# A decoder trunk on one core: the mLSTM gate chain spread over early column pairs, two sums in place, other last pairs, and the first head's q and k split before the head stage

## The chip, the core and the metric

The kernel runs on one core of a Trainium2 chip. A core has TensorE (PE, matmuls), VectorE (DVE), ScalarE (ACT), GpSimd (POOL) and SyncE (SP), which issues nearly all DMAs of this kernel. Each engine works through its own instructions in order and waits on semaphores for the others. The metric is the device time of one execution in microseconds; the number shown for a kernel is the median of several executions.

## What is computed

One layer of a hybrid trunk on 512 tokens of width 2048, in float32:

```python
x = x + mixer(rms_norm(x, norm_mix0))
x = x + swiglu_ffn(rms_norm(x, norm_ffn0))
return rms_norm(x, final_norm)

def mlstm_retention_mixer(h, w_in, b_gates, w_conv, g_ml, g_ret, w_out):
    proj = h @ w_in                     # 2048 x (8 * 1024 + 8)
    ml_qk, ml_v, ml_o, r_q, r_k, r_v, r_g, gates = split(proj)
    ml_qk = silu(causal_conv(ml_qk, w_conv))
    i_pre, f_pre = split(gates + b_gates)
    h_ml = mlstm_chunkwise(ml_q, ml_k, ml_v, i_pre, f_pre)        # 4 heads of 256
    h_ml = head_norm(h_ml, g_ml) * sigmoid(ml_o)
    h_ret = retention_chunkwise(rotary(r_q), rotary(r_k), r_v)    # 4 heads of 256
    h_ret = head_norm(h_ret, g_ret, center=True) * silu(r_g)
    return concat(h_ml, h_ret) @ w_out
```

The gates of the mLSTM go through a log-sigmoid, a cumulative sum in each chunk of 128 tokens, and a running maximum over the chunks.

## The kernel before

All matrices are held transposed: 128 channels on the partitions, 512 tokens along the free dimension. A float32 product is made of fp32r parts: `split` (L80) writes a weight tile's rounded half `whi` with a cast on ACT (L84) and the rest `wlo` with a subtraction on DVE (L85).

**Projection.** `w_in` is taken in 32 column pairs of 256 columns. The pair number says what it holds: 0 to 3 mLSTM q, 4 to 7 mLSTM k, 8 to 11 mLSTM v, 12 to 15 the output gate (normed, sigmoid), 16 to 19 retention q and 20 to 23 retention k (rotary), 24 to 27 retention v, 28 to 31 the retention gate (normed, Silu). Two pairs go plainly with the gate columns; the other 30 go through `strassen` (L198), in the order of the list in L291. Such a pair takes seven products of 16 matmuls (A11, A12, S2, S1, S3, S4, A22; L209, L210, L213), in PSUM banks a, b and c. The weights of a product are a block as loaded (`b11`, `b21`, `b12`, `b22`) or a sum that `added` (L220) makes: q1, t2, t4, t3. S3 accumulates on top of S2's bank, which ACT has copied out at L246 by then. The results are collected on ACT and DVE (L241 to L261); `done` (L429) scales, rotates or gates them and stores them to a scratch tensor `pd` in HBM.

`r4` (L63) gives tiles of 512 KB from a pool of ten slots, which all of this shares: blocks, sums, the tables of cosine and sine, the gates' tiles, and later the residual stream.

**Gates.** `gates` (L371), behind the last pair, is a chain of small operations on 4 partitions: bias, |f|, exp, ln, a correction with a reciprocal (L388), scans for each chunk (L402 to L407), an exponential (L411), two stores of rows, and four PE transposes (L416), whose results are copied into `cols` (L421).

**Heads.** Four retention heads and four mLSTM heads follow. A retention head loads k, q, v and its gate from `pd` (`load`, L486; tiles `ld` with four buffers, or `ahead` for the first head), splits k and q (`two_parts`, L508), transposes v on PE and scales it on ACT (L503), and makes scores (L528), which DVE multiplies by a decay table `dec` (L615). Two banks `tp` serve both transposes and scores. The numerators (L544) are copied out on ACT (L626). Output-projection steps (`residual_gemm`, L129) are filled in between. The tiles of the head stage lie where the projection's operands lay, so they can be written only when the last pairs have been multiplied.

**Order.** The code is written in program order, but a scheduler lists the instructions of each engine by its own reckoning of priorities, slots and durations. The order in which instructions stand on an engine is therefore read from the built program.

Of the kernel before, what the change touches and what calls it, by code (L numbers as in the profile page):

```python
# [33 lines left out]
WU = 1024  # L34
# [4 lines left out]
def trunk(ctx: ExitStack, tc: tile.TileContext, xT, xr, w_in, w_gate, w_out, w_gu, w_down, w_pairs,  # L39
# [23 lines left out]
    def r4(shape, dtype=F32):  # L63
        return rp.tile(shape, dtype, name="r4")
# [133 lines left out]
    def strassen(j, src, cbs, ep, psp, done, between=None):  # L198
# [21 lines left out]
        def added(x, y):  # L220
            t = r4([P, WU])[:, 0:n_k * P]
            nc.vector.tensor_add(t, x, y)  # L222
            return t
# [23 lines left out]
        t4 = added(t2, b21)  # L247
        product(c, split(q1), S1, True)
        nc.scalar.copy(two[:, 0], c)
        t3 = added(b12, b22)  # L250
# [32 lines left out]
    xq = xT.rearrange("(n q p) t -> q p n t", n=2, p=P)  # L283
    pd = dram.tile([32, P, 2, T], F32, name="pd")
    rows = dram.tile([2, NH, T], F32, name="rows")
    with ExitStack() as proj:
# [4 lines left out]
        order = [24, 25, 26, 27, 16, 0, 4, 20, 8, 1, 5, 17, 2, 9, 6, 21, 3, 10, 18, 7, 28, 11, 22, 29, 30, 19, 31, 12, 23, 13, 14, 15]  # L291
# [79 lines left out]
        def gates():  # L371
            space = [r4([36, 2, T]) for _ in range(3)]
            st = space[0][:, 0, :]
            e, u, lg, d, f = (x[0:NH, n, :] for x, n in ((space[0], 1), (space[1], 0), (space[1], 1),
                                                         (space[2], 0), (space[2], 1)))
            gsum = gate_rows[0]
            fr, ig = gsum, gsum[0:NH, :]
# [6 lines left out]
            nc.scalar.activation(e, e, AF.Exp, scale=-1.0)  # L384
            nc.vector.tensor_scalar_add(u, e, 1.0)
            nc.scalar.activation(lg, u, AF.Ln)
            nc.vector.scalar_tensor_tensor(out=d, in0=u, scalar=-1.0, in1=e, op0=ALU.add, op1=ALU.subtract)
            nc.vector.reciprocal(u, u)  # L388
            nc.vector.tensor_mul(d, d, u)
            nc.vector.tensor_sub(lg, lg, d)  # L390
            lf = e
            nc.vector.scalar_tensor_tensor(out=lf, in0=f, scalar=0.0, in1=lg, op0=ALU.min, op1=ALU.subtract)

            b, c, m = f, u, lg
            carry = const.tile([NH, NC + 1], F32, name="carry", tag="warm")
            nc.vector.memset(carry, 0.0)

            nc.gpsimd.memset(st, 0.0)
            for i in range(NC):
                s = slice(i * CH, (i + 1) * CH)  # L400
                last = slice((i + 1) * CH - 1, (i + 1) * CH)
                nc.vector.tensor_tensor_scan(out=b[:, s], data0=ones[0:NH, :], data1=lf[:, s], initial=0.0,  # L402
                                             op0=ALU.mult, op1=ALU.add)
                nc.vector.tensor_sub(c[:, s], ig[:, s], b[:, s])
                nc.vector.tensor_tensor_scan(out=m[:, s], data0=c[:, s], data1=c[:, s],
                                             initial=carry[:, i:i + 1], op0=ALU.max, op1=ALU.max)
                nc.vector.tensor_add(carry[:, i + 1:i + 2], b[:, last], m[:, last])  # L407
            nc.vector.tensor_copy(st[0:NH, :], c)
            bm = d
# [3 lines left out]
            nc.sync.dma_start(out=rows[1], in_=b)  # L413
            tp = psp.tile([P, T], F32, name="aux")
# [54 lines left out]
        all_pairs([(w_in[n], stored(n)) for n in order[2:]], cbs, ep, psp, {0: normalise}, plain_done)  # L469
        gates()  # L470
# [7 lines left out]
    with ExitStack() as mix:  # L478
        hp = mix.enter_context(tc.tile_pool(name="hp", bufs=1, reuse_waits="tile"))
        ahead = {}  # L480
        for n in (20, 16, 24):
            ahead[n] = r4([P, 2, T])
            nc.sync.dma_start(out=ahead[n], in_=pd[n])
# [24 lines left out]
        def two_parts(t, name):  # L508
            hi, lo = (hp.tile([P, 2, T], F32R, name=name + x, bufs=2) for x in "hl")
            nc.scalar.copy(hi, t)  # L510
            nc.vector.tensor_tensor(out=lo, in0=t, in1=hi.bitcast(F32), op=ALU.subtract)
            return hi, lo
# [93 lines left out]
        def retention_head(h, pool, out):  # L606
            kT = two_parts(load(20 + h), "kT")
            qT = two_parts(load(16 + h), "qT")
# [297 lines left out]
```

## Time and profile before

| | us |
|---|---|
| median of three runs | 2297.26 |
| lowest and highest | 2295.38, 2298.49 |
| the profiled execution | 2298.28 |
| its span, first to last instruction | 2296.2 |

| engine | busy us of the span |
|---|---|
| PE | 2252.6 (98%) |
| DVE | 2004.8 (87%) |
| ACT | 1177.2 (51%) |
| POOL | 45.2 (2%) |

Times in views are microseconds from the span's start. The projection's pairs run until about 660, the heads until about 920, then the FFN. In a table of stretches each engine has its busy time and count, then the granted clock of PE as a share of full speed and the share of the DMA engines. In a timeline a row has a start, a length, and in brackets how long the engine stood idle before it and what released it. Matmuls are pipelined: a row's length is longer than the step to the next row.

### The profile page before, as it was taken

Reading aid. Unit: us, or ns where it says so; the run is one execution under the profiler, and the core shown is the slowest. Engines: PE = TensorE matmul, PEld = TensorE weight load, DVE = VectorE, ACT = ScalarE, POOL = GpSimd, SP = SyncE. Lnnn points to the kernel's source line nnn. Section 1 sums busy time; section 2 is a strip of 40 time slices with the busy share of each in tenths; the row PEclk is TensorE's granted clock in tenths of the full one; section 3 lists DMA queues with packets and bytes.
Section 4 is the critical chain, followed back from the end, with each engine's and each line's share of the span. In section 5 each row is a group of like instructions: output and inputs, shape, how many; then the busy total and the mean of one; then the engine's idle time right before and its main releaser. Section 6 shows DMA issues by size and latency. Waiting matters only on the chain.

```text
span 2296.2 us, 31553 instructions
## 1 busy us (share of the span) xinstructions
PE 2252.6 (98%) x12264; PEld 1937.6 (84%) x12264; DVE 2004.8 (87%) x2454; ACT 1177.2 (51%) x1569; POOL 45.2 (2%) x48
## 2 busy tenths in 40 slices
PE   9999999999989999799999999999999999999997
PEld 7888888888878888688888888888888888888887
DVE  6898988989987976999899999999999899898685
ACT  6544444545567744554545445454445545545233
POOL 0000000000000001300000000000000000000000
PEclk9999999999999999999999999999999999999999
DMA  8444334443374523333333333333333664864752
GB/s 267 155 139 137 130 129 130 137 137 128 130 243 160 159 92 122 144 122 117 117 123 124 124 124 121 114 115 124 124 116 120 209 229 149 270 204 150 271 205 74
DMA packets 140806, 343.59 MB, mean 150 GB/s; under 512 B 12264, under 2 KB 60648, under 8 KB 140656
## 3 DMA queue, kind: packets, MB, share of 16 engines
q1 hardware_dynamic: 140656, 341.57, 45.0%
q8 instruction: 96, 1.57, 0.3%
q14 instruction: 54, 0.44, 0.1%
HBM read 288.03 MB, written 53.49 MB: 149 GB/s over the span
## 4 chain that ended last, share of the span: by engine, by line
PE 90%; DVE 5%; DMA 2%; ACT 2%; issue 1%; POOL 1%; SPq 0%; DVEq 0%; POOLq 0%; ACTq 0%
PE a L210 27%; PE c L210 14%; PE a L213 12%; PE b L210 7%; PE c L213 6%; PE b L213 3%; PE mm L91 3%; PE mm L89 3%; PE mm L90 3%; PE a L209 2%; PE c L209 1%; DVE wlo L85 1%; PE c L89 1%; PE c L90 1%; PE c L91 1%
## 5 line engine op out<-in xcount | busy, mean ns | idle before, releaser
L210 PE MATMUL a<-cb,whi 128*128 128x512 f32 x2572 | 926.9, 398 | 4.0 <-DVE cb L155 4.0
L213 PE MATMUL a<-cb,wlo 128*128 128x256 f32 x2242 | 630.6, 281 | 0.5 <-DVE wlo L85 0.4
L210 PEld LDWEIGHTS a<-cb,whi 128*128 128x128 f32 x2572 | 480.0, 189 | 92.6 <-DVE cb L155 4.6
L85 DVE TENSOR_TENSOR wlo<-r,whi 128x1024 fp32r<-128x1024 f32 (+1 forms) x412 | 491.5, 1195 | 58.5 <-ACT whi L84 56.5
L84 ACT CAST whi<-r 128x1024 fp32r<-128x1024 f32 (+1 forms) x412 | 424.6, 1032 | 104.7 <-PE b L210 60.6
L210 PE MATMUL c<-cb,whi 128*128 128x512 f32 x1280 | 465.7, 397 | 0.2 <-ACT whi L84 0.2
L213 PEld LDWEIGHTS a<-cb,wlo 128*128 128x128 f32 x2242 | 424.5, 189 | 17.2 <-DVE wlo L85 2.2
L84 ACT CAST whi<-raw 128x1024 fp32r<-128x1024 f32 (+1 forms) x234 | 242.4, 1036 | 331.8 <-PE c L210 126.4
L85 DVE TENSOR_TENSOR wlo<-raw,whi 128x1024 fp32r<-128x1024 f32 (+1 forms) x234 | 281.2, 1202 | 38.0 <-ACT whi L84 37.5
L213 PE MATMUL c<-cb,wlo 128*128 128x256 f32 x1116 | 313.0, 280 | 0.0
L210 PEld LDWEIGHTS c<-cb,whi 128*128 128x128 f32 x1280 | 240.9, 188 | 44.0 <-ACT whi L84 0.6
L222 DVE TENSOR_TENSOR r<-r,r 128x1024 f32<-128x1024 f32 (+1 forms) x184 | 215.7, 1173 | 20.1 <-DMA r<-in_w_gu 17.2
L210 PE MATMUL b<-cb,whi 128*128 128x512 f32 x628 | 229.7, 399 | 0.0
L213 PEld LDWEIGHTS c<-cb,wlo 128*128 128x128 f32 x1116 | 210.8, 189 | 7.3 <-DVE wlo L85 0.2
L213 PE MATMUL b<-cb,wlo 128*128 128x256 f32 x548 | 154.4, 282 | 0.8 <-DVE wlo L85 0.8
L210 PEld LDWEIGHTS b<-cb,whi 128*128 128x128 f32 x628 | 118.9, 189 | 21.8
L261 DVE TENSOR_TENSOR e<-e 128x512 f32<-128x512 f32 x180 | 123.5, 688 | 9.2 <-ACT e L258 7.3
L258 ACT COPY e<-a 128x512 f32<-128x512 f32 x90 | 52.9, 588 | 146.1 <-PE a L210 146.1
L246 ACT COPY e<-a 128x512 f32<-128x512 f32 x90 | 53.0, 588 | 143.9 <-PE a L210 136.8
L222 DVE TENSOR_TENSOR r<-raw,r 128x1024 f32<-128x1024 f32 (+1 forms) x90 | 105.7, 1175 | 6.5 <-DMA r<-in_w_gu 2.9
L213 PEld LDWEIGHTS b<-cb,wlo 128*128 128x128 f32 x548 | 104.2, 190 | 4.5 <-DVE wlo L85 1.1
L89 PE MATMUL mm<-hi,whi 128*128 128x512 f32 x256 | 101.4, 398 | 3.2 <-DVE r L139 2.9
(289 smaller groups left out, 3350.1 us busy)
## 6 DMA issues: line engine op xcount, KB each, us to landing
r<-in_w_gu SPq DMA_DIRECT2D x89, 512.0 KB, 4.1
raw<-in_w_gu SPq DMA_DIRECT2D x87, 512.0 KB, 3.2
raw<-in_w_in SPq DMA_DIRECT2D x67, 512.0 KB, 3.5
r<-in_w_in SPq DMA_DIRECT2D x61, 512.0 KB, 3.7
raw<-in_w_down SPq DMA_DIRECT2D x40, 512.0 KB, 4.4
pd<-e SPq DMA_DIRECT2D x64, 256.0 KB, 2.7
raw<-in_w_out SPq DMA_DIRECT2D x32, 512.0 KB, 3.3
ld<-pd SPq DMA_DIRECT2D x29, 512.0 KB, 4.1
```

The source lines that it names most:

```text
L84: nc.scalar.copy(hi, raw)
L85: nc.vector.tensor_tensor(out=lo, in0=raw, in1=hi.bitcast(F32), op=ALU.subtract)
L89: nc.tensor.matmul(acc, wh, xh, start=first, stop=False)
L90: nc.tensor.matmul(acc, wh, xl, start=False, stop=False)
L91: nc.tensor.matmul(acc, wl, xh, start=False, stop=last)
L209: nc.tensor.matmul(*small, start=False, stop=False, skip_group_check=not first)
L210: nc.tensor.matmul(acc, wh[:, ks], cbs[k][:, c, :, :], start=(first and k == 0), stop=last, skip_group_check=not first)
L213: nc.tensor.matmul(*small, start=False, stop=False, skip_group_check=not first)
L222: nc.vector.tensor_add(t, x, y)
L246: nc.scalar.copy(two[:, 1], a)
L258: nc.scalar.copy(one[:, 0], a)
L261: nc.vector.tensor_add(x[:, :, 0, :], x[:, :, 0, :], x[:, :, 1, :])
```

## The change

- `gates` is cut into seven pieces, which are called between products of pairs 0, 2 to 10 of the 30 (`between`, L251); its reciprocal is made in two halves and its scans in two halves. The operations are the same.
- `added` may write into one of its inputs: t4 overwrites t2 and t3 overwrites b12.
- The order of pairs changes: 12 to 15 take the places of 9, 10, 11 and so on, so that the last two pairs are 10 and 11, which are stored as they are.
- The first head's k (pair 20) and q (pair 16) are loaded and split into `r4` tiles before the projection's pools close, and its v (pair 24) is loaded there.

```diff
-        def added(x, y):
-            t = r4([P, WU])[:, 0:n_k * P]
+        def added(x, y, into=None):
+            t = r4([P, WU])[:, 0:n_k * P] if into is None else into
             nc.vector.tensor_add(t, x, y)
             return t
...
-        t4 = added(t2, b21)
+        t4 = added(t2, b21, t2)
...
-        t3 = added(b12, b22)
+        t3 = added(b12, b22, b12)
...
-        order = [24, 25, 26, 27, 16, 0, 4, 20, 8, 1, 5, 17, 2, 9, 6, 21, 3, 10, 18, 7, 28, 11, 22, 29, 30, 19, 31, 12, 23, 13, 14, 15]
+        order = [24, 25, 26, 27, 16, 0, 4, 20, 8, 1, 5, 17, 2, 12, 6, 21, 3, 13, 18, 7, 28, 9, 22, 29, 30, 19, 31, 14, 23, 15, 10, 11]
...
-            nc.vector.reciprocal(u, u)
+
+        def gates_3(n):
+            half = gs["u"][:, n * HT:(n + 1) * HT]
+            nc.vector.reciprocal(half, half)
...
-            for i in range(NC):
+        def gates_5(n):
+            lf, b, c, m, ig, carry = (gs[x] for x in ("e", "f", "u", "lg", "ig", "carry"))
+            for i in range(2 * n, 2 * n + 2):
...
-        all_pairs([(w_in[n], stored(n)) for n in order[2:]], cbs, ep, psp, {0: normalise}, plain_done)
-        gates()
+        all_pairs([(w_in[n], stored(n)) for n in order[2:]], cbs, ep, psp,
+                  {0: normalise, 2: gates_1, 3: gates_2, 4: lambda: gates_3(0), 5: lambda: gates_3(1), 6: gates_4,
+                   7: lambda: gates_5(0), 8: lambda: gates_5(1), 9: gates_6, 10: gates_7}, plain_done)
+
+        for n in (20, 16):
+            x, hi, lo = r4([P, 2, T]), r4([P, 2, T], F32R), r4([P, 2, T], F32R)
+            nc.sync.dma_start(out=x, in_=pd[n])
+            nc.scalar.copy(hi, x)
+            nc.vector.tensor_tensor(out=lo, in0=x, in1=hi.bitcast(F32), op=ALU.subtract)
+            first_parts[n] = hi, lo
+        ahead[24] = r4([P, 2, T])
+        nc.sync.dma_start(out=ahead[24], in_=pd[24])
...
-        ahead = {}
-        for n in (20, 16, 24):
-            ahead[n] = r4([P, 2, T])
-            nc.sync.dma_start(out=ahead[n], in_=pd[n])
...
-            kT = two_parts(load(20 + h), "kT")
-            qT = two_parts(load(16 + h), "qT")
+            kT = first_parts.get(20 + h) or two_parts(load(20 + h), "kT")
+            qT = first_parts.get(16 + h) or two_parts(load(16 + h), "qT")
```

How the built programs stand at three places. First ACT at the end of the projection, in the kernel before (e_5705 and e_5706 are the results of the last pair, r_5830 the gates' tile, kTh and qTh the casts of k and q):

```order
L84 CAST whi<-raw 128x1024 x2
L258 COPY e_5705<-a 128x512
L446 ACTIVATE e_5706<-e_5706 128x2x256
L510 CAST kTh<-r_5889 128x1024
L411 ACT_TABLE_LOAD
L411 ACTIVATE r_5830<-r_5832 4x512
L446 ACT_TABLE_LOAD
L446 ACTIVATE e_5705<-e_5705 128x2x256
L510 CAST qTh<-r_5891 128x1024
L503 ACTIVATE v<-tp,rs 128x128 x8
```

and in the changed kernel (e_5699 is a result of the last pair, L528 what L503 was, L535 what L510 was, L651 what L626 was):

```order
L84 CAST whi<-raw 128x1024 x2
L258 COPY e_5699<-a 128x512
L84 CAST whi<-raw 128x1024
L528 ACTIVATE v<-tp,rs 128x128 x8
L535 CAST kTh<-ld 128x1024
L535 CAST qTh<-ld 128x1024
L651 COPY hn<-num 128x256 x2
```

The exponential, the sigmoids, the two casts and the table loads no longer stand between the last copy and the scaling of v; a weight cast does.

Second the DMA queue of SP at the same place, before (L490 loads for heads, L427 stores of the last pair, L612 decay tables, L654 residual, L75 weights of the output projection):

```order
L75 DMA raw<-in_w_out 128x1024
L412 DMA rows<-r_5831 4x512
L490 DMA ld<-pd 128x1024
L427 DMA pd<-e_5706 128x2x256
L612 DMA dec<-in_decay 128x512
L490 DMA ld<-pd 128x1024 x2
L427 DMA pd<-e_5705 128x2x256
L490 DMA ld<-pd 128x1024
L612 DMA dec<-in_decay 128x512
```

and changed (L515 loads for heads, L446 stores, L637 decay tables, L679 residual):

```order
L679 DMA r_6159<-in_xT 128x2x512
L75 DMA raw<-in_w_out 128x1024
L446 DMA pd<-e_5700 128x2x256
L75 DMA raw<-in_w_out 128x1024
L446 DMA pd<-e_5699 128x2x256
L515 DMA ld<-pd 128x1024
L637 DMA dec<-in_decay 128x512
L515 DMA ld<-pd 128x1024 x3
L637 DMA dec<-in_decay 128x512 x2
```

The first load for a head and the first decay table now stand behind both stores of the last pair, and the value load of the second head no longer stands behind one of them.

Third PE in a pair, at the end of product S2 (bank a) and the start of S1 (bank c), as it stands there in the kernel before:

```order
L209 MATMUL a<-cb,wlo 128x256
L210 MATMUL a<-cb,whi 128x512
L210 MATMUL c<-cb,whi 128x512
L213 MATMUL c<-cb,wlo 128x256
L210 MATMUL c<-cb,whi 128x512
```

and in pair 10 of the changed kernel (L435 is what L416 was):

```order
L209 MATMUL a<-cb,wlo 128x256
L210 MATMUL a<-cb,whi 128x512
L210 MATMUL c<-cb,whi 128x512
L435 MATMUL aux<-ident,r_1017 128x36 x4
L210 MATMUL a<-cb,whi 128x512
L213 MATMUL c<-cb,wlo 128x256
L210 MATMUL c<-cb,whi 128x512
```

Here the first matmul of S3 (bank a again) stands before the rest of S1; it does so in pairs 1, 3 and 27 too, there without L435 between.

## Rows read from the trace of the kernel before

**Rows 1.** The page, busy time and share of the span by engine.

```profile
PE 2252.6 (98%) x12264; PEld 1937.6 (84%) x12264; DVE 2004.8 (87%) x2454; ACT 1177.2 (51%) x1569; POOL 45.2 (2%) x48
```

**Rows 2.** Stretches: length, busy (count) of PE, PEld, DVE, ACT, POOL, clock, DMA.

```profile
110.00:300.00 190.00, 190.00 (x1079) 164.89 (x1078) 173.91 (x184) 90.15 (x107) 0.00 (x0) 1.00 0.42 140
...
640.00:660.00 20.00, 19.88 (x112) 16.76 (x111) 19.97 (x36) 11.67 (x15) 0.14 (x2) 1.00 0.71 217
...
664.00:672.00 8.00, 6.18 (x21) 5.13 (x22) 3.08 (x6) 7.21 (x14) 0.00 (x0) 0.50 0.94 329
```

**Rows 3.** Timeline of PE from the last projection matmul to the third head.

```profile
659.53 0.39 PE L210 MATMUL a<-cb,whi 128*128 128x512 f32 x1
664.44 0.64 PE L416 MATMUL aux<-ident,r 36*128 36x36 f32 x4 [4.52 <-ACT r L411]
665.01 1.97 PE L501 MATMUL tp<-ident,r 128*128 128x128 f32 x8
668.36 0.80 PE L89 MATMUL tp<-qTh,kTh 128*128 128x512 f32 x1 [1.39 <-ACT v L503]
...
676.83 0.50 PE L89 MATMUL tp<-qTh,kTh 128*128 128x512 f32 x1 [0.36 <-ACT v L503]
...
687.92 1.03 PE L501 MATMUL tp<-ident,ld 128*128 128x128 f32 x8
```

**Rows 4.** Chain that ended last, 655 to 700: start, step, what.

```profile
657.13 1.14 DVE wlo L85
658.27 0.60 DVE e L256
...
691.38 0.23 PE tp L90
...
692.71 0.17 PE tp L90
...
693.72 0.12 PE tp L90
```

**Rows 5.** Timeline of ACT, in a pair and behind the last one.

```profile
648.99 0.59 ACT L246 COPY e<-a 128x512 f32<-128x512 f32 x1 [1.21 <-PE a L210]
...
659.96 0.59 ACT L258 COPY e<-a 128x512 f32<-128x512 f32 x1 [1.76 <-PE a L210]
...
662.46 1.28 ACT L411 ACT_TABLE_LOAD   x1
663.75 0.63 ACT L411 ACTIVATE r<-r 4x512 f32<-4x512 f32 x1
...
667.17 2.17 ACT L503 ACTIVATE v<-tp,rs 128x128 f32<-128x128 f32 x8
669.85 1.05 ACT L510 CAST kTh<-ld 128x1024 fp32r<-128x1024 f32 x1 [0.51 <-DMA ld<-pd]
671.15 1.05 ACT L510 CAST qTh<-ld 128x1024 fp32r<-128x1024 f32 x1 [0.25 <-DMA ld<-pd]
```

**Rows 6.** Timeline of SP's DMA queue: start and length of the issues.

```profile
661.54 0.37 SPq L427 DMA_DIRECT2D pd<-e  x1
661.96 0.46 SPq L612 DMA_DIRECT2D dec<-in_decay  x1
662.47 0.92 SPq L490 DMA_DIRECT2D ld<-pd  x2
```

**Rows 7.** Issue to landing: median of all loads, spread of the decay tables.

```profile
ld<-pd SPq DMA_DIRECT2D x29, 512.0 KB, 4.1
...
DMA to landing us min/median/max: 4.1/5.2/6.2
```

**Rows 8.** Who PE waited for between 660 and 860: total, times, longest.

```profile
PE tp L89 <- ACT v L503: 2.1, 4, 1.4
```

**Rows 9.** DVE's groups from 629 to 662; the largest and smallest of the gates' twelve.

```profile
L388 DVE RECIPROCAL r<-r 4x512 f32<-4x512 f32 x1 | 3.3, 3329 | 0.0
...
L408 DVE COPY r<-r 4x512 f32<-4x512 f32 x1 | 0.4, 407 | 0.0
```

More of the change, by code (lines that the diff above doesn't have):

```diff
@@ L283, in trunk @@
     xq = xT.rearrange("(n q p) t -> q p n t", n=2, p=P)
+    ahead, first_parts = {}, {}
     pd = dram.tile([32, P, 2, T], F32, name="pd")
@@ L368, in normalise, with gates_1 @@
             nc.vector.tensor_mul(gsum, gsum, rb[0:36, :])
-        def gates():
+        gs = {}
+        def gates_1():
             space = [r4([36, 2, T]) for _ in range(3)]
[L373 to L377, printed above, removed]
+            gs["st"] = space[0][:, 0, :]
+            for n, x in (("e", space[0][:, 1, :]), ("u", space[1][:, 0, :]), ("lg", space[1][:, 1, :]),
+                         ("d", space[2][:, 0, :]), ("f", space[2][:, 1, :])):
+                gs[n] = x[0:NH, :]
+            e, f, fr = gs["e"], gs["f"], gate_rows[0]
+            ig = gs["ig"] = fr[0:NH, :]
             nc.vector.tensor_scalar(out=ig, in0=ig, scalar1=bg[0:NH, :], scalar2=None, op0=ALU.add)
@@ L384, in gates, with gates_2 @@
             nc.scalar.activation(e, e, AF.Exp, scale=-1.0)
+        def gates_2():
+            e, u, lg, d = (gs[n] for n in ("e", "u", "lg", "d"))
             nc.vector.tensor_scalar_add(u, e, 1.0)
@@ L387, in gates, with gates_4 @@
             nc.vector.scalar_tensor_tensor(out=d, in0=u, scalar=-1.0, in1=e, op0=ALU.add, op1=ALU.subtract)
-            nc.vector.reciprocal(u, u)
+        def gates_3(n):
+            half = gs["u"][:, n * HT:(n + 1) * HT]
+            nc.vector.reciprocal(half, half)
+        def gates_4():
+            e, u, lg, d, f = (gs[n] for n in ("e", "u", "lg", "d", "f"))
             nc.vector.tensor_mul(d, d, u)
             nc.vector.tensor_sub(lg, lg, d)
[L391 to L395, printed above, removed]
+            nc.vector.scalar_tensor_tensor(out=e, in0=f, scalar=0.0, in1=lg, op0=ALU.min, op1=ALU.subtract)
+            carry = gs["carry"] = const.tile([NH, NC + 1], F32, name="carry", tag="warm")
             nc.vector.memset(carry, 0.0)
-            nc.gpsimd.memset(st, 0.0)
-            for i in range(NC):
+            nc.gpsimd.memset(gs["st"], 0.0)
+        def gates_5(n):
+            lf, b, c, m, ig, carry = (gs[x] for x in ("e", "f", "u", "lg", "ig", "carry"))
+            for i in range(2 * n, 2 * n + 2):
                 s = slice(i * CH, (i + 1) * CH)
@@ L407, in gates, with gates_6 @@
                 nc.vector.tensor_add(carry[:, i + 1:i + 2], b[:, last], m[:, last])
+        def gates_6():
+            b, c, m, bm, st = (gs[x] for x in ("f", "u", "lg", "d", "st"))
             nc.vector.tensor_copy(st[0:NH, :], c)
-            bm = d
             nc.vector.tensor_add(bm, b, m)
@@ L413, in gates, with gates_7 @@
             nc.sync.dma_start(out=rows[1], in_=b)
+        def gates_7():
+            st = gs["st"]
             tp = psp.tile([P, T], F32, name="aux")
```

## Prediction

> **What bounds the kernel now.** I read the page's busy shares first, then a table of stretches, then the stretch in which TensorE (PE) stands still. PE is busy for 2252.6 of 2296.2 us [rows 1], so anything that does not shorten its work can give back at most the other 43.6 us, and only where PE waits. In the projection pairs it does not wait at all: 190.00 us of the 190 from 110 to 300, at a granted clock of 1.00, with VectorE (DVE) at 173.91 [rows 2]. So the whole projection is PE work, and moving DVE work about in it gains nothing there; it can only cost.
>
> The place that the change aims at is the end of the projection. The last projection matmul ends at 659.53 + 0.39 = 659.92 us (T from here on) and PE then stands 4.52 us, until the exponential of the gate chain has released its four transposes [rows 3]. The chain of waits can be followed back on ScalarE (ACT): the exponential runs at 663.75, behind a table load, a sigmoid and a cast [rows 5]. Eight transposes of the values follow, then 1.39 us of waiting for ACT to scale them, then the scores of the first head from 668.36 [rows 3]. Meanwhile the clock has fallen: 0.50 from 664 to 672, with PE busy for 6.18 of the 8 us [rows 2]. The second head's first score comes at 676.83, after another 0.36 us [rows 3], that is T + 16.91. What PE did in between would take, at the steps of a full clock, 6 x 0.23 + 6 x 0.17 + 12 x 0.12 = 3.8 us of scores [rows 4], 2 x 1.03 of transposes [rows 3], some 0.3 for the gates' four and about 1.3 for six value products: 7.5 us. So 9.4 us of these 16.91 are waits and half clock. This is the whole prize; up to 860 the waits for scaled values, the largest kind that is left, come to 2.1 us in four places, most of it the 1.39 and 0.36 already counted [rows 8].
>
> **The change part by part.**
>
> *The gate chain among early pairs.* It leaves the path at T: the 4.52 us wait, the exponential, its table loads and the sigmoid of the last pair (now a pair without one) are gone from ACT behind T. Its DVE work is 12 groups of rows from 3.3 us (the reciprocal) down to 0.4, in sum 12.5 us [rows 9], and now lies in pairs 2 to 10. DVE has 190 - 173.91 = 16.1 us idle in the 190 us of about those pairs [rows 2]; with 12.5 and some 1.3 for a pair that now has a norm there, it is left with 2.3. That it can be full without PE waiting is shown between 640 and 660: DVE 19.97 of 20, and PE is busy until T (19.88) [rows 2]. But that was 20 us, not 180, and in the two rotary pairs the margin is small: counting the order's rows of pair 7 and 8 at 1.14 us a split and 0.60 an addition [rows 4], the split that the second product needs is ready about 0.3 us before PE wants it. I take 0.5 us of PE waiting in all; bounds 0 (as 640 to 660) and 12.5 (every piece waited for, which the 2.3 us of margin speak against); for the range I use 3. The three gate tiles hold 3 of the 10 slots; the loads then come one after another, but each still some 10 us before its product, so I cost them at nothing. If that cover failed each of nine pairs would wait for part of a 4 us load.
>
> *The two sums in place* are the same additions on the same engine: nothing gained or lost in time. They free two of six slots per pair, which the gate and first-head tiles take.
>
> *The scheduler's answer.* The order of the new kernel has a thing that the diff does not show. At four places (pairs 1, 3, 10 and 27) PE is given the first matmul of the third product right after one matmul of the second. The third product accumulates into the bank that ACT must first copy out (L246). In the kernel before, a whole product of matmuls covers that copy, and ACT waits for PE, not PE for ACT (the copy at 648.99 stands idle 1.21 us before it, then takes 0.59) [rows 5]. Now PE stands from the end of the first product to the end of the copy: about 0.04 + 0.59 + 0.08 - 0.23 of the one matmul between = 0.48 us, three times, and 0.2 where the gates' transposes lie between (these cost 0.3 of PE wherever they lie): 1.6 us. Bounds: 0 if PE's queue hides it, 0.7 each = 2.8.
>
> *The handover at T.* The q and k of the first head are split before T, so PE goes straight on: eight transposes end at T + 1.1. ACT first evacuates the last accumulator, then, in the new order, casts a weight tile before it scales the values: 0.5 + 1.05, and then four of eight scalings, 2.17 / 2 [rows 5]. The first score can start at T + 2.8 (before T + 8.44), and two rows of scores end by T + 5.3. The next needs the decay table. Its DMA stands behind the last store and one load on the SP queue, where the store waits for the last sum: T + 0.6 + 0.65 for copy and sum, then issues of 0.37 + 0.33, so it goes out at about T + 2.1, the next three loads at T + 2.6, 3.1 and 3.6 (issues of 0.46 each) [rows 6]. A decay table landed after 4.1 to 6.2 us [rows 7]; with the residual's loads partly done before T I take 4.5: T + 6.6, then some 0.7 of DVE for 512 columns (an addition of that width steps by 0.60 [rows 4]), and scores again from T + 7.3.
>
> The second head is then what is late next. Its k and q were issued at 662.47 and cast at 669.85 and 671.15, right after landing: 7.4 us and about 8.2 in the crowd [rows 5, 6]; the median load of this kind takes 4.1 [rows 7]. Fewer residual loads stand beside them now, so I take 6.1 for q, the middle: T + 9.2, and T + 10.3 for the values. ACT stands in order: cast of q (1.05) until T + 10.3, the numerators' copies until T + 10.9, during which PE waits for a numerator bank; the transposes then end at T + 11.9 and, with half of the scaling under them, the second head's first score starts at about T + 12.6. Gain: 16.9 - 12.6 = 4.3 us. Bounds: with loads at their median 4.1 it would be T + 10.3 (gain 6.6); with loads as in the crowd and a clock that falls once more, T + 15.5 (gain 1.4).
>
> The Trainium skill ("DMA: Bandwidth & Descriptors", section "Latency and other measured facts") says that the fixed cost of a DMA shrinks under a lighter load of the memory, and its section "Anatomy of one DMA" gives about 2.0 us plus bytes / 436 GB/s. An estimate from that page for the decay table is 2.6 us, landing at T + 4.7 instead of 6.6; the second head's first score would hardly move, since q lands later. This case's decay tables, at 4.1 us and more [rows 7], do not reach that figure.
>
> *The clock.* It fell in a wait of 4.52 us; waits of 1.39 and 0.36 us, the second at full clock, stand beside it [rows 2, 3]. The longest waits that I now expect are 1.7 to 2 us with matmuls between. I take no loss, with 1 us as the upper bound (in the bounds above), since half of the matmuls lie under waits for DMA anyway.
>
> *Behind it* I take the rest as unchanged, give or take 1.5 us: the same matmuls in another order, one residual load less behind T.
>
> **Sum against the profiled execution** (2298.28 us, span 2296.2): - 4.3 (handover) + 0.3 (transposes among the pairs; they were inside the 16.9) + 1.6 (early first matmuls) + 0.5 (DVE) = - 1.9 us, so 2296.4. The median of the three runs is 2297.26, 1.0 lower than that execution; so I predict 2295.4.
>
> **The rivals.**
>
> *A, the handover pays in full.* Loads land at their median and PE's queue hides three of the four early matmuls: - 6.6 + 0.3 + 0.5 + 0 = - 5.8, 2291.5. For it: fewer bytes beside the loads; against it: 0.94 DMA share between 664 and 672 before [rows 2], and the in-order ACT.
>
> *B, slower: DVE becomes the bound of pairs 2 to 10.* If the DVE rows cannot be closed up as between 640 and 660, because splits wait for casts, PE waits for most pieces: 12.5 + 1.3 us of new work against the idle that can really be used. It decides when less than about 5 of the 16.1 us are usable: then PE loses 9 us, less 4.3 for the handover, plus 0.3 + 1.6: + 6.6, about 2303.9. Against it: the idle between 110 and 300 is spread over all pairs, and 640 to 660 shows it used up.
>
> *C, the wait only changes hands.* The loads of the second head land as late as before, since they could never start before T: gain 1.4 to 2, minus 2.4: about 2297.5, no change.
>
> **How the numbers follow.** Forecast 0.54, A 0.28, B 0.08, C 0.10. A difference of 0.2% (4.6 us, below 2292.7 or above 2301.9) is about what a measurement of this kernel can tell from no change. A alone is faster, B alone slower: 0.28 / 0.64 / 0.08. The range: down to 2290.0 (A with half a microsecond of luck behind it) and up to 2299.5 (the forecast with 3 us of DVE waiting and a late load), which leaves out B and about a tenth.
>
> **What would show it.** In the new trace: no wait for an exponential at the end of the projection, first score within 3 us of T, second head's first score at T + 12 to 13, PE waits there named after the decay table's multiplication and the numerators' copies; at pairs 1, 3, 10 and 27 gaps of 0.2 to 0.5 us that end with ACT L246; DVE over 95% busy from 110 to 300. Wrong if PE loses over 3 us before T (then B), if the second head starts at T + 15 (C) or before T + 11 (A), or if the clock stays half for more than 4 us.

## The result: slower, and the profile after

The changed kernel took 2309.66 us (median of 6 runs, 2308.42 to 2311.97) beside 2297.68 us for the kernel before on the same chip (2295.38 to 2300.06): a ratio of 1.0051, 95% interval 1.0041 to 1.0061. The forecast was 2295.4 with a range up to 2299.5, so both the sign and the range were missed. The profiled execution took 2308.42 us with a span of 2306.6, that is 10.4 us more than the span before. The busy shares of the page (as [rows 1]):

```profile
PE 2257.7 (98%) x12264; PEld 1936.3 (84%) x12264; DVE 2002.3 (87%) x2455; ACT 1177.5 (51%) x1565; POOL 47.6 (2%) x48
```

PE's work is the same number of instructions. Three stretches tell where 10.4 us are: T, the end of the last projection matmul, moves from 659.92 to 665.96 (+6.0); from T to the first matmul of the feed-forward stage's norm (L109) it takes 297.97 instead of 293.04 (+4.9); the rest takes 1342.7 instead of 1343.2 (-0.5). Against the forecast's terms: the part up to T was to lose 2.4 us and lost 6.0; the second head's first score was to come 4.3 us earlier behind T and came 1.0 earlier; from there to the L109 matmul was to stay the same, give or take 1.5, and takes 282.0 us instead of 276.1 (+5.9).

**In the projection.** The stretch that stood without a PE gap before [rows 2] now has some (columns as there):

```profile
110.00:300.00 190.00, 188.05 (x1063) 161.65 (x1062) 176.58 (x207) 92.18 (x111) 0.00 (x0) 1.00 0.41 138
```

PE lost 1.95 us there, at a full clock. Whom it waited for from 80 to 665 us, from the view of waits (us in total, times, longest):

```profile
PE a L210 <- ACT e L246: 1.6, 3, 0.7
PE c L213 <- DVE wlo L85: 0.9, 1, 0.9
PE a L210 <- DVE e L254: 0.5, 2, 0.3
PE a L213 <- DVE wlo L85: 0.4, 1, 0.4
```

The first row is the early first matmul of the third product (S3). One of these places, PE first and then ACT:

```profile
614.12 0.40 PE L210 MATMUL c<-cb,whi 128*128 128x512 f32 x1
614.96 0.49 PE L210 MATMUL a<-cb,whi 128*128 128x512 f32 x1 [0.44 <-ACT e L246]
...
614.32 0.58 ACT L246 COPY e<-a 128x512 f32<-128x512 f32 x1 [1.76 <-PE a L210]
```

From one start to the next 0.84 us pass; a step without a wait is about 0.23, so a gap shown as 0.44 costs 0.61, and the next step (to 615.42) is longer too. The other thing that is new stands on DVE, between 80 and 650 us. Its waits for weight loads before and after:

```profile
DVE r L222 <- DMA r<-in_w_in: 1.1, 2, 0.6
```

```profile
DVE r L222 <- DMA r<-in_w_in: 20.9, 20, 2.6
DVE r L222 <- DMA raw<-in_w_in: 3.9, 7, 1.2
```

The sums (L222) now wait 24.8 us for loads where they waited 1.1. DVE works in order, so the splits and subtractions behind them stand too.

**At the handover.** PE's timeline (as [rows 3]):

```profile
665.56 0.40 PE L210 MATMUL a<-cb,whi 128*128 128x512 f32 x1
665.80 1.03 PE L526 MATMUL tp<-ident,r 128*128 128x128 f32 x8
668.62 0.50 PE L89 MATMUL tp<-r,r 128*128 128x512 f32 x1 [1.79 <-ACT v L528]
...
671.00 0.34 PE L91 MATMUL tp<-r,r 128*128 128x384 f32 x1
674.69 0.39 PE L89 MATMUL tp<-r,r 128*128 128x256 f32 x1 [3.35 <-DVE w L640]
...
681.89 0.50 PE L89 MATMUL tp<-qTh,kTh 128*128 128x512 f32 x1
...
690.96 1.74 PE L569 MATMUL num<-v,w 128*128 128x256 f32 x6 [2.78 <-ACT hn L651]
```

The wait for the gate chain is gone and the first score comes at T + 2.66. Then PE stands 3.35 us for the decay table's multiplication. The second head starts at 681.89, T + 15.93: of the 16.91 before, 1.0 us is won. DVE, SP's DMA queue and ACT in this stretch (as [rows 6] and [rows 5]):

```profile
673.94 1.16 DVE L640 TENSOR_TENSOR w<-tp,dec 128x512 f32<-128x512 f32 x2 [5.16 <-DMA dec<-in_decay]
...
668.31 0.38 SPq L637 DMA_DIRECT2D dec<-in_decay  x1
668.74 1.93 SPq L515 DMA_DIRECT2D ld<-pd  x3
670.71 7.24 SPq L637 DMA_DIRECT2D dec<-in_decay  x2
...
675.15 1.04 ACT L535 CAST kTh<-ld 128x1024 fp32r<-128x1024 f32 x1 [5.55 <-DMA ld<-pd]
676.43 1.04 ACT L535 CAST qTh<-ld 128x1024 fp32r<-128x1024 f32 x1 [0.24 <-DMA ld<-pd]
```

The table left at 668.31 (T + 2.35) and was there 5.6 us later. On SP the third head's table waits until about 678 for a buffer that the first head's table still holds, with the third head's loads queued behind it. The clock was at half level for 3.41 us from 675.15 on, right behind the 3.35 us of standing still, and again for 3.41 us from 692.22 on, behind the 2.78 us wait in the last row of PE's timeline. PE's steps show it: 0.21 us for 256 columns instead of 0.12.

### The profile page after: what moved, and what is told of

Same layout as the page of the kernel before. It is cut to its first block, busy times and chain, and to the rows that moved or that the text cites. A ratio compares the mean times of both kernels' runs of the same rounds, so it can differ in the third digit from the quotient of the medians.

```text
span 2306.6 us, 31696 instructions
## 1 busy us (share of the span) xinstructions
PE 2257.7 (98%) x12264; PEld 1936.3 (84%) x12264; DVE 2002.3 (87%) x2455; ACT 1177.5 (51%) x1565; POOL 47.6 (2%) x48
## 4 chain that ended last, share of the span: by engine, by line
PE 80%; DVE 10%; DMA 4%; issue 2%; ACT 2%; POOL 1%; SPq 0%; DVEq 0%; POOLq 0%; ACTq 0%
PE a L210 25%; PE c L210 12%; PE a L213 11%; PE b L210 6%; PE c L213 5%; DVE wlo L85 3%; PE b L213 3%; PE mm L91 2%; PE mm L89 2%; PE mm L90 2%; DMA r<-in_w_in 2%; PE a L209 2%; DVE z L547 1%; PE c L209 1%; DVE r L222 1%
## 5 line engine op out<-in xcount | busy, mean ns | idle before, releaser
L222 DVE TENSOR_TENSOR r<-r,r 128x1024 f32<-128x1024 f32 (+1 forms) x184 | 214.6, 1171 | 17.0 <-DMA r<-in_w_in 15.2
L222 DVE TENSOR_TENSOR r<-raw,r 128x1024 f32<-128x1024 f32 (+1 forms) x90 | 105.7, 1175 | 41.8 <-DMA raw<-in_w_gu 29.2
L246 ACT COPY e<-a 128x512 f32<-128x512 f32 x90 | 52.8, 587 | 145.9 <-PE a L210 145.9
L249 ACT COPY e<-c 128x512 f32<-128x512 f32 x90 | 52.8, 587 | 107.7 <-PE c L210 107.7
```

The costliest lines, as they stand in the source:

```text
L246: nc.scalar.copy(two[:, 1], a)
```

## The experiments

All medians are beside the kernel before on the same chip. "Pairs" is the time from the norm's row matmul in the first pair (L118, at 82.33 us before) to T; "heads" is the time from T to the feed-forward stage's L109. The stretches are read from one profiled execution of each kernel.

| kernel | median us | ratio (95%) | pairs | first score | heads |
|---|---|---|---|---|---|
| before | 2297.7 | 1 | 577.6 | T + 8.4 | 293.0 |
| changed | 2309.7 | 1.0051 (1.0041 to 1.0061) | 583.9 | T + 2.7 | 298.0 |
| before, both sums in place | 2319.6 | 1.0099 (1.0084 to 1.0114) | 588.7 | T + 8.5 | 303.3 |
| before, only t4 over t2 | 2299.6 | 1.0011 (1.0001 to 1.0020) | 577.9 | T + 8.7 | 293.0 |
| before, only t3 over b12 | 2299.1 | 1.0003 (0.9993 to 1.0012) | 576.4 | T + 8.4 | 292.9 |
| before, new pair order | 2297.6 | 0.9998 (0.9989 to 1.0008) | 577.1 | T + 6.0 | 292.9 |
| changed, gates behind the pairs | 2314.2 | 1.0071 (1.0056 to 1.0086) | 586.5 | T + 6.5 | 298.7 |
| changed, first head as before | 2312.4 | 1.0065 (1.0050 to 1.0080) | 584.9 | T + 3.6 | 301.6 |
| changed, own tiles for the sums | 2304.4 | 1.0022 (1.0011 to 1.0032) | 579.3 | T + 2.7 | 297.5 |
| same, t4 over t2 | 2304.4 | 1.0024 (1.0015 to 1.0034) | 579.1 | T + 2.7 | 297.8 |
| own tiles, early decay table | 2297.3 | 0.9992 (0.9983 to 1.0002) | 579.2 | T + 2.7 | 290.7 |
| same, gates spread over 4 to 24 | 2296.7 | 0.9994 (0.9984 to 1.0003) | 579.1 | T + 2.7 | 289.8 |
| same, gates behind the pairs | 2306.1 | 1.0036 (1.0023 to 1.0049) | 577.1 | T + 6.5 | 302.0 |
| changed, early decay table | 2301.9 | 1.0012 (1.0002 to 1.0022) | 584.9 | T + 2.7 | 290.2 |

Three more runs on the sums are told with their numbers below. As a measure of what a stretch can tell: the four kernels in which PE waits nowhere between 100 and 656 us (before, only t3 over b12, new pair order, and the one with own tiles, early table and the gates behind the pairs) have pairs of 576.4 to 577.6. The intervals of the ratios reach some 0.001 either way, that is about 2 us.

### The parts of the change one by one

Only the two sums in place:

```diff
-        t4 = added(t2, b21)
+        t4 = added(t2, b21, t2)
-        t3 = added(b12, b22)
+        t3 = added(b12, b22, b12)
```

> The kernel before with the two sums written in place, and nothing else. Theory S (the in-place sums cost the projection its 6 us: in the built order the first matmul of the third product stands before the rest of the second one, and t4 can be added only behind the split of t2): nine such places at 0.5 to 0.9 us, so the last projection matmul ends 4 to 9 us later than 659.9, and the whole is 4 to 9 us slower. Theory G (the gate pieces on VectorE cost it): the last projection matmul ends within 1.5 us of 659.9 and the whole is within 2 us of the kernel before.

Measured: 21.8 us slower, 11.1 of them in the pairs and 10.2 in the heads: more than either theory allowed (4 to 9, or under 2), with the gaps of theory S. PE, DVE and the queue in one pair of it:

```profile
194.86 0.50 PE L210 MATMUL a<-cb,whi 128*128 128x512 f32 x1 [0.44 <-ACT e L246]
...
203.78 0.47 PE L210 MATMUL a<-cb,whi 128*128 128x512 f32 x1 [0.48 <-DVE e L254]
...
194.67 2.35 DVE L85 TENSOR_TENSOR wlo<-r,whi 128x1024 fp32r<-128x1024 f32 x2
200.67 1.23 DVE L222 TENSOR_TENSOR r<-raw,r 128x1024 f32<-128x1024 f32 x1 [3.65 <-DMA r<-in_w_in]
201.81 1.22 DVE L85 TENSOR_TENSOR wlo<-r,whi 128x1024 fp32r<-128x1024 f32 x1
202.95 0.68 DVE L254 TENSOR_TENSOR e<-e,a 128x512 f32<-128x512 f32 x1
...
194.77 1.46 SPq L217 DMA_DIRECT2D r<-in_w_in  x2
```

DVE stands 3.65 us for a load issued at 194.77; the split and the subtraction L254 behind it come late, and PE waits 0.48 us for L254. Between 80 and 650 us such waits for loads come to 34.1 us:

```profile
DVE r L222 <- DMA r<-in_w_in: 29.3, 22, 3.7
DVE r L222 <- DMA raw<-in_w_in: 4.8, 4, 1.9
```

The new pair order alone, on the kernel before:

```diff
-order = [24, 25, 26, 27, 16, 0, 4, 20, 8, 1, 5, 17, 2, 9, 6, 21, 3, 10, 18, 7, 28, 11, 22, 29, 30, 19, 31, 12, 23, 13, 14, 15]
+order = [24, 25, 26, 27, 16, 0, 4, 20, 8, 1, 5, 17, 2, 12, 6, 21, 3, 13, 18, 7, 28, 9, 22, 29, 30, 19, 31, 14, 23, 15, 10, 11]
```

> The kernel before with the new order of pairs alone (gates still behind the last pair). Both theories: the projection ends at 660 as before. The wait for the gates' exponential stays, but no sigmoid and fewer table loads stand behind it on ScalarE: 0 to 3 us faster in the handover; if the other order of the head stage alone brings the 5 us that the changed kernel loses there, it is 2 to 5 us slower instead.

It costs nothing: the time is within its interval of no change. The first score comes 2.4 us earlier, and nothing of that reaches the feed-forward stage.

The changed kernel with the gate pieces called behind the last pair:

```diff
-                  {0: normalise, 2: gates_1, 3: gates_2, 4: lambda: gates_3(0), 5: lambda: gates_3(1), 6: gates_4,
-                   7: lambda: gates_5(0), 8: lambda: gates_5(1), 9: gates_6, 10: gates_7}, plain_done)
+                  {0: normalise}, plain_done)
+        for g in (gates_1, gates_2, lambda: gates_3(0), lambda: gates_3(1), gates_4, lambda: gates_5(0),
+                  lambda: gates_5(1), gates_6, gates_7):
+            g()
```

> The changed kernel with its gate pieces called one after another behind the last pair. Theory S: the projection ends 4 to 9 us later than in the kernel before, as in the one with the sums in place alone, and the wait for the exponential (4 to 5 us) comes back: 2311 to 2316. Theory G: the projection ends at 660 to 662 and the whole is at 2303 to 2308.

The changed kernel with the first head's q, k and v loaded in the head stage, as before:

```diff
-        for n in (20, 16):
-            x, hi, lo = r4([P, 2, T]), r4([P, 2, T], F32R), r4([P, 2, T], F32R)
...
+        for n in (20, 16, 24):
+            ahead[n] = r4([P, 2, T])
+            nc.sync.dma_start(out=ahead[n], in_=pd[n])
```

> The changed kernel with the first head's q, k and v loaded as in the kernel before and split in the head stage. Theory S and G: the projection ends at 666 as in the changed kernel. If the early split gains what it was credited with (first score 5.8 us earlier, second head 1 us earlier), this one is 1 to 3 us slower than the changed kernel; if the slots and the queue order of the early split cost the head stage its 4.9 us, it is 3 to 6 us faster than the changed kernel.

Both times came out as the first range of their expectation said (2314.2 us; 2.8 us slower than the changed kernel). With the gate pieces behind the last pair the pairs are not shorter but 2.6 us longer; the order is another, and PE waits for L246 at nine early first matmuls, 4.2 us, in place of three, 1.6 us. With the first head loaded and split as before the wait for the decay table is still there, 3.20 us, and the heads are longer still. So neither the gate pieces nor the early split was the main cost.

### Which of the sums, and why

On the kernel before, each line of that diff alone, first t4's:

> The kernel before with t4 alone written over t2. Theory S1 (only both sums in place together bring the third product's first matmul forward; this order has no such place): within 2 us of the kernel before. Theory S2 (it is t4, which has to wait behind the split of t2 and pushes other VectorE work back): 4 us or more slower, with waits for VectorE in the pairs.

then t3's:

> The kernel before with t3 alone written over b12. In the built order the first matmul of the second product stands after the first one of S2 in nine pairs, which needs no copy of a bank. Theory S1: within 2 us of the kernel before. Rival: t3 in place is what costs: 4 us or more slower.

The sums alone in place cost 1.7 and 1.2 us by the medians (the first just clear of nothing, the second within its interval of it), and neither shows in the pairs, 577.9 and 576.4 us, or in the heads. On this kernel the price is one of the two together. In the changed kernel, both put back:

```diff
-        t4 = added(t2, b21, t2)
+        t4 = added(t2, b21)
-        t3 = added(b12, b22, b12)
+        t3 = added(b12, b22)
```

> The changed kernel with the two sums in tiles of their own again (gate pieces, new order and early split kept). Theory S (the sums in place cost both the projection and, through the order that follows, the heads): last projection matmul at 660 to 662, from there to the first sum of squares of the FFN 288 to 293 us, the whole 2290 to 2297. Theory G (gate pieces or slots): last matmul still at 665 or later, since 11 tiles now want 10 slots and loads come later; the whole 2308 or more.

and the second line of that alone:

> The changed kernel with t3 in a tile of its own and t4 still over t2; one place in the order where the third product's first matmul comes early instead of four. Theory S1: last projection matmul at 660 to 662.5, and the whole 3 to 12 us faster than the changed kernel. Theory G: last matmul at 664 or later, the whole within 3 us of the changed kernel.

Both sums back in tiles of their own give 5.2 us back, 4.6 of it in the pairs. That lies between the theories: T is at 662.73, and 2304.4 us is above the 2297 that theory S allowed, since the heads stay at 297.5. With t4 over t2 and only t3 in a tile of its own the time is the same, so on the changed kernel it is t3 over b12 beside t4 over t2 that costs; t3 alone was not run there.

Two more tries ask what it is about the two together. The first writes t3 over q1's tile, which frees as many slots:

```diff
         t4 = added(t2, b21, t2)
-        t3 = added(b12, b22, b12)
+        t3 = added(b12, b22, q1)
```

on the kernel before and on the changed one:

> The kernel before with both weight sums written over a tile that is already there: the one ahead of the fourth product over t2, as in the change, and the one ahead of the third product over q1's tile, where the change takes the tile of b12. As many slots come free as in the run that had only the two sums in place (2319.6 us). In the order of this kernel no first matmul of the third product stands early on TensorE; in that run it stood early at about ten places. Theory S (what costs is the order that the scheduler gives when this pair of tiles is reused, not that sums are written in place): within 3 us of before, 2295 to 2301, the last projection matmul at 659 to 662 us, no gap of 0.4 us that ends with ACT L246. Rival (sums written over their own operand, or the slots that come free and the loads that they let go early, cost by themselves): 2310 or more, the last projection matmul at 666 or later.

> The changed kernel with one word different: the sum ahead of the third product is written over q1's tile and not over b12's. Theory S: the early first matmuls at three pairs go, some 2.8 us; the waits for the gate pieces (some 2.2 us) stay, so the last projection matmul ends at 662 to 663.5, and the whole takes 2304 to 2307. Rival (the order is not it): within 1.5 us of the changed kernel, 2308 to 2311.

Measured: 2314.5 us (1.0071, 1.0056 to 1.0086) on the kernel before, T at 670.48, and 2319.9 us (1.0097, 1.0082 to 1.0112) on the changed one, T at 672.14. My theory, that the cost hangs on the early first matmuls that this one choice of tiles brings, falls. In the run on the kernel before none of them is left, and DVE waits for loads only 2.0 us in three places. PE waits for something else, mainly this (waits from 100 to 656 us):

```profile
PE a L213 <- DVE wlo L85: 4.7, 8, 0.8
```

In the run on the changed kernel it is mainly the same wait, at ten places between 80 and 672 us, 4.7 us in all. DVE's timeline of one pair of the run on the kernel before shows why:

```profile
195.74 1.21 DVE L85 TENSOR_TENSOR wlo<-r,whi 128x1024 fp32r<-128x1024 f32 x1
196.99 1.22 DVE L222 TENSOR_TENSOR r<-r,r 128x1024 f32<-128x1024 f32 x1
199.66 2.36 DVE L85 TENSOR_TENSOR wlo<-r,whi 128x1024 fp32r<-128x1024 f32 x2 [1.45 <-ACT whi L84]
```

The sum at 196.99 overwrites q1, so it must stand behind q1's split at 195.74. Its own cast on ACT and its split follow at 198.58 and 199.66, one after the other, and PE, which is at that product by 199.70, waits until 200.94. In the kernel before t3 has a tile of its own and is formed a pair ahead: the sum at 197.82 here is the next pair's, and this pair's split at 196.69 waits for no sum.

```profile
196.69 1.22 DVE L85 TENSOR_TENSOR wlo<-r,whi 128x1024 fp32r<-128x1024 f32 x1
197.82 1.22 DVE L222 TENSOR_TENSOR r<-r,r 128x1024 f32<-128x1024 f32 x1
```

The second run keeps the sums in place but lets the pool of slots turn as fast as before:

```diff
         t4 = added(t2, b21, t2)
+        nc.gpsimd.memset(r4([P, WU])[:, 0:1], 0.0)
         ...
         t3 = added(b12, b22, b12)
+        nc.gpsimd.memset(r4([P, WU])[:, 0:1], 0.0)
```

> The run with only the two sums in place, and beside each of them a tile that GpSimd clears one column of and nobody reads, so that the pool of ten slots turns as fast as in the kernel before and no load may go earlier than there by a free slot. Theory O (a sum that is written over its operand stands elsewhere in the scheduler's order: the next pair's sums on VectorE early, the third product's first matmul on TensorE early at some nine places; that order costs): 2313 to 2322, the last projection matmul at 666 to 670, gaps of 0.44 us that end with ACT L246 at eight or more pairs. Rival (the free slots and the loads that they let go cost): 2297 to 2303, the last projection matmul below 662.

Measured: 2319.5 us (1.0094, 1.0079 to 1.0109), pairs 588.8, and the waits for L246 are there as in the run with the sums in place alone; so are DVE's for loads:

```profile
PE a L210 <- ACT e L246: 3.5, 8, 0.4
```

```profile
DVE r L222 <- DMA r<-in_w_in: 30.5, 19, 3.8
```

The freed slots are not it. What is left is the order, and it can be read in the built programs. DVE of the kernel before, behind the split of b22 for the fourth product (S4):

```
L85 TENSOR_TENSOR wlo_2290<-r4_2222,whi_2289 128x1024
L254 TENSOR_TENSOR e4_2194<-e4_2194,a_2144 128x512
L222 TENSOR_TENSOR r4_2549<-raw_2488,r4_2492 128x1024
```

and with the two sums in place:

```
L222 TENSOR_TENSOR r4_2527<-raw_2466,r4_2470 128x1024
L222 TENSOR_TENSOR r4_2470<-r4_2470,r4_2472 128x1024
L85 TENSOR_TENSOR wlo_2270<-r4_2181,whi_2269 128x1024
L254 TENSOR_TENSOR e4_2176<-e4_2176,a_2126 128x512
```

Before, this pair's last split and its subtraction L254 come first, and then q1 of the pair after next. Now q1, and in place behind it t3, of the pair after next stand ahead of both. They need that pair's loads, which have often not landed, and PE waits for the split and the subtraction. Counted from 0 among the 30 pairs, q1 stands so early in pairs 2 to 27 of that program and in pairs 8 to 27 of the changed kernel, and in none of the kernel before. That this order costs the time is read from the programs and the waits; no run kept the sums in place and changed only the order. With t3 over q1's tile q1 stands early too, but there its loads have mostly landed, and the price comes by the other way shown above.

### The decay table

The first head's table, loaded ahead of T into a tile of its own, on the kernel with own tiles and on the changed one:

```diff
+        first_dec = r4([P, NC * CH])
+        nc.sync.dma_start(out=first_dec, in_=decay[0])
...
-            dec = hp.tile([P, NC * CH], F32, name="dec", tag="dm", bufs=2)
-            nc.sync.dma_start(out=dec, in_=decay[h])
+            dec = first_dec
+            if h > 0:
+                dec = hp.tile([P, NC * CH], F32, name="dec", tag="dm", bufs=2)
+                nc.sync.dma_start(out=dec, in_=decay[h])
```

> The changed kernel with both sums in tiles of their own (2304.4 us) and with the first head's decay table loaded ahead of the end of the projection, so that the wait of 3.4 us of TensorE behind the first two rows of scores has no cause. Theory L (the second head's loads, which cannot start before the last projection matmul, set when the second head starts): the wait of the first head goes, the second head's first score stays at 15 to 16 us behind the last projection matmul, the feed-forward stage starts 296.5 to 298 behind it, and the time is within 1.5 us of 2304.4. Rival (the decay table's wait is what holds ScalarE and TensorE back): the second head's first score at 12 to 13, and 2300.5 to 2302.

> The changed kernel with one thing different: the first head's decay table is loaded ahead of the end of the projection. If its wait (3.35 us of TensorE, with ScalarE's casts and the next decay load queued behind it) is what took the handover's gain: the second head's first score 13 to 13.5 us behind the last projection matmul (15.93 in the changed kernel), the feed-forward stage 290.5 to 293 behind it (297.97), the last projection matmul at 666 as in the changed kernel, the time 2302 to 2305. Rival (the second head's loads or the sums in place hold the head stage back): 15 or more, 296 or more, 2308 or more.

Measured: 7.1 us less than without it on the kernel with own tiles, and 7.7 less on the changed kernel, whose pairs stay within 1 us (584.9 beside 583.9); the heads go from 297.5 and 298.0 to 290.7 and 290.2. My theory here, that the second head's loads set its start anyway, falls; the rival's 2300.5 to 2302 is passed too. PE in the changed kernel with the early table:

```profile
668.64 0.50 PE L89 MATMUL tp<-r,r 128*128 128x512 f32 x1 [1.79 <-ACT v L530]
...
676.32 1.56 PE L571 MATMUL num<-v,w 128*128 128x256 f32 x6 [0.93 <-ACT hn L655]
...
679.55 0.50 PE L89 MATMUL tp<-qTh,kTh 128*128 128x512 f32 x1 [0.36 <-ACT v L530]
```

ACT in the same run, then the stretch from T to the second head's start (columns as [rows 2], the last one GB/s), first with the early table and then in the changed kernel:

```profile
674.95 1.04 ACT L537 CAST kTh<-ld 128x1024 fp32r<-128x1024 f32 x1 [1.55 <-DMA ld<-pd]
```

```profile
666.00:679.50 13.50, 10.47 (x60) 8.66 (x58) 8.05 (x15) 7.84 (x20) 0.11 (x1) 1.00 0.81 288
```

```profile
666.00:681.90 15.90, 10.50 (x53) 8.49 (x51) 6.97 (x12) 7.64 (x19) 0.00 (x0) 0.89 0.82 276
```

The loads come no earlier: the second head's k is cast at 674.95 with the early table and at 675.15 without. Yet the head starts at T + 13.58 instead of T + 15.93, since PE has the first head's scores and most of its values behind it when the loads land. The granted clock falls nowhere between T and 940 us, where the changed kernel has two half stretches. Up to the second head's start PE was busy for 10.47 of 13.5 us, at a clock of 1.00; in the changed kernel for 10.50 of 15.9, at 0.89. The third head's first score is at T + 25.0 instead of T + 29.7. The edit does a second thing there: the first table no longer takes one of the two buffers of `dec`, so the third head's table no longer holds the queue, and that head's loads go out 1.5 to 2.1 us earlier (677.28 to 679.24 instead of 678.75 to 681.30). How much of the 7 us is this and how much the first table's own wait was not separated.

### The gate pieces

In the run with own tiles and early table, the pieces at other pairs:

```diff
-                  {0: normalise, 2: gates_1, 3: gates_2, 4: lambda: gates_3(0), 5: lambda: gates_3(1), 6: gates_4,
-                   7: lambda: gates_5(0), 8: lambda: gates_5(1), 9: gates_6, 10: gates_7}, plain_done)
+                  {0: normalise, 4: gates_1, 6: gates_2, 8: lambda: gates_3(0), 11: lambda: gates_3(1), 14: gates_4,
+                   16: lambda: gates_5(0), 19: lambda: gates_5(1), 22: gates_6, 24: gates_7}, plain_done)
```

> The run with the early decay table, and the gate pieces at every second or third pair from 4 to 24 in place of every pair from 2 to 10. If the pieces cost because they crowd VectorE in neighbouring pairs: the waits for VectorE L85 and L254 (some 2.2 us in the changed kernel) go, the last projection matmul ends at 660 to 661, about 2 us earlier than with the pieces in pairs 2 to 10, and the whole is 2 us below that run. Rival (each piece costs what it takes of VectorE wherever it stands, since VectorE has no idle that can be used): the last projection matmul at 662.5 or later, no gain.

and all of them behind the last pair:

> The run with both sums in tiles of their own and the early decay table (2297.3 us), with the gate pieces put back behind the last pair. If the gates' place is worth what it gives at the handover: the first score 6 to 6.5 us behind the last projection matmul (2.66 with the pieces among the pairs), the second head's first score at 15.5 to 17 (13.15), the last projection matmul at 659.5 to 661 (661.4), the time 2299 to 2302. Rival (the second head's loads arrive meanwhile, so that the gates' wait is under theirs): the second head's first score at 13 to 14.5, the time 2295 to 2297.5.

The pieces among the pairs cost 2.1 us there (579.2 against 577.1, one execution each), and spreading them changes nothing (579.1): T is at 660.74, as the first theory wanted, but only because the kernel was earlier at the mark. Between 100 and 656 us PE waits for DVE twice in either, and not at all with the pieces behind the pairs. Here with the pieces in pairs 2 to 10:

```profile
PE a L210 <- DVE e L254: 0.6, 1, 0.6
PE a L213 <- DVE wlo L85: 0.3, 1, 0.3
```

With the pieces behind the pairs the first score (T + 6.5) and the second head's (T + 16.1) come as expected, but the heads take 302.0, more than before the change, so that the move is worth 8.8 us there and not 2 to 5. Of the 11.3 us that the heads are longer, PE stands idle for 6.4 (27.2 us beside 20.8) and is busy 4.9 longer (274.8 beside 269.9) for the same work, with the clock at half level for 18.9 us beside 9.3. Why the later heads wait more in that order I did not take apart; ACT, DVE and SP have other orders there too. The same holds for the 10 us that the sums in place alone cost in the heads: PE's idle time there is 29.7 us beside 22.1 before, with one new wait of 4.5 us for a cast of q (L510) and 7.2 us instead of 2.1 for scaled values (L503). The two best runs, with the pieces in pairs 2 to 10 and spread, are 0.9992 and 0.9994 of before: no difference that the intervals show.

## Why the prediction was wrong

Step by step, against what the prediction put:

- **The two sums in place, "nothing gained or lost in time": this step failed.** The additions themselves cost the same. But a sum written over an operand may only stand behind the last reader of it, and the scheduler wrote another order on DVE and PE. In the changed kernel it costs 4.6 us in the pairs and 5.2 us in all; on the kernel before 21.8 us. That alone would turn the forecast's -1.9 us into +3.3. It is not alone in this: the handover, below, missed by more, and with either of the two put right the kernel is still slower than before (1.0022 and 1.0012).
- **The early first matmuls (+1.6).** Right in kind and place (three gaps that end with ACT L246, and a smaller one in pair 10, at 276 us), low in size: 0.7 to 0.8 us each with what the steps lose beside the gap and 0.4 in pair 10, some 2.7 us, near the upper bound of 2.8. I took them for the whole of the scheduler's answer. The other part, DVE's sums ahead of loads that have not landed, was in the same order and I did not look for it: loads "at nothing" became 24.8 us of DVE waits.
- **The gate pieces (+0.5).** Mis-sized: 2.1 us in all where the sums have their own tiles, against 0.5 + 0.3. DVE over 95% busy from 110 to 300 did not come (176.58 of 190 is 93%); rival B's bound was not reached.
- **The handover (-4.3).** The path up to the first score (2.8, measured 2.66) and the end of two rows of scores (5.3, measured 5.4) were right. The decay table was mis-sized: issued at T + 2.35 for 2.1, but 5.6 us under way where I took 4.5, under the median of 5.2 in the spread that stood there [rows 7], so that PE stood 3.35 us and not 2.0. The fit in the Trainium skill ("DMA: Bandwidth & Descriptors", section "Anatomy of one DMA") makes 2.6 us of it, an estimate; but that fit is for DMAs that GpSimd issues, and this one went out on SP's queue, where the trace has 5.6. Then "I take no loss" for the clock failed: a wait of that length was followed by half clock. q was cast at T + 10.5 for an expected 9.2. The second head came at T + 15.9, 0.4 us beyond the worst bound I gave (15.5). With the early table it comes at T + 13.2 to 13.6: 3.3 to 3.8 of the 4.3 us.
- **Behind the handover "unchanged, give or take 1.5".** Failed: from the second head's first score to the L109 matmul it took 5.9 us more. Three things are new there: the second half clock, the wait of 2.78 us for ACT at 690.96, and SP's queue held for a decay buffer; what each costs was not separated. With the early table, which also frees that buffer, the same stretch takes 276.7 us, 0.5 more than before.
- **The rivals.** C named the outcome at the handover (the wait changes hands; the second head at T + 15), but for the wrong reason: the loads do land late, and still the table was what held. B's time came nearer than my own (2303.9), also not by its mechanism. Forecast and rivals alike lacked a case in which the sums in place reorder the pairs. Two of the prediction's own signs of being wrong came true: PE lost over 3 us before T, though not for B's reason, and the second head started later than T + 15.

Summed up by differences of runs: of the 12.0 us that the change costs, the sums in place are 5.2 and the decay table 7.1 (its wait and the buffer together), each to within some 3 us by the intervals of the ratios. Without both, the rest of the change stood 0.9 us below the kernel before (2297.3 beside 2298.2), which the interval can't tell from nothing, where I had forecast 1.9 below.

## What to carry to other kernels

Writing a result over its operand adds a dependence, and where a scheduler orders the engines that dependence decides where the instruction stands: read the order of every engine at such places, above all whether an in-order engine now gets work that needs a load ahead of work that a matmul needs. When a long wait is taken off a path, list each transfer that the old wait hid and charge it at the slow end of what the trace shows for such transfers in that stretch. Price a remaining wait with the clock that follows it, not by its length alone.

## What the runs showed of the hardware that I had not expected

A decay table of 256 KB took 5.6 us and the 512 KB loads of `ld` beside it 5.4 to 8.0 us from issue, where the stretch moved 276 GB/s in the mean; the median of such loads over the whole kernel before was 4.1 us [rows 7]. In the changed kernel a PE wait of 3.35 us was followed by 3.41 us at 1.2 GHz, and one of 2.78 us by as much again, while waits of 1.79 and 0.93 us in the run with the early table left the clock at 2.4 GHz.
